# A float32 encoder trunk on one core: gate rows multiplied and split in two lots of four, later pieces of x asked for one block sooner, the residual asked for behind the last key block's weights

## The chip, the core and the metric

The kernel runs on one core of one Trainium2 chip. The metric is the device time of one execution in microseconds (us), less is better. The engines that matter are TensorE (PE; its weight loads are PEld), VectorE (DVE), ScalarE (ACT), GpSimd (POOL) and SyncE (SP), which issues nearly all transfers. [...]

## The reference

Two layers over x (256 tokens, 2048 features, float32). Cut to what matters here:

```python
for l in range(DEPTH):                                   # DEPTH = 2
    h = rms_norm(x, norm1_g[l])
    q, k, v, gu, gv = jnp.split(h @ w_in[l], splits, axis=-1)
    q = apply_rope(rms_norm(q.reshape(B, S, 8, 128), q_norm_g[l]), cos, sin)
    k = apply_rope(rms_norm(k.reshape(B, S, 2, 128), k_norm_g[l]), cos, sin)
    attn = banded_window_attention(q, k, v, sink[l])     # softmax with a sink logit per head
    sgu = chunked_spatial_gating(gelu(gu), gelu(gv), ...)   # gu * (w_s @ layer_norm(gv) + b_s)
    mixed = concatenate([rms_norm(attn, attn_out_g[l]), rms_norm(sgu, sgu_out_g[l])])
    x = x + mixed @ w_o[l]
    x = x + conv_gated_ffn(rms_norm(x, norm2_g[l]), w_up[l], conv_w[l], conv_b[l], w_down[l])
```

## The kernel before, in words

**Products in parts.** Every float32 factor is split in a high part (rounded to fp32r) and a low part (the rest), and a product is three matmuls: high by high, low by high, high by low. Weights come from HBM in blocks of 1 MB (128 x 2048) into four `raw` tiles. ACT copies the high part into `his`, DVE subtracts it and writes the low part into `los` (`lo_part`, L149). For the row products (`rows_by_cols`, L203 for the matmuls by the high part, L208 for those by the low part) a block is split in two halves of 128 x 1024, and `his` and `los` have four such places in a ring: a place is written again when PE has read it. A block covers four key tiles of 128; each takes four L203 and two L208 matmuls of 512 columns.

**Activations.** Left factors are also split, by `split_act`: ACT writes gain times value as the high part (L359), DVE the low part (L360). `first_rows(b)` does so for block b of x in the first layer: x transposed comes in pieces of 256 KB (`in_xT`, L675; the first four smaller, L106).

**The first stage.** In layer 0 the keys and values (`psk`) and the first queries (`psq`) are built side by side over four blocks b of the features (`NB` = 4). Around them stand: a load of the rope tables, of the row `qk` (gains of q and k and the sinks, copied to all partitions, L454) and of the rest of the column parameters, all three issued by ACT and tied by `issue_after` behind the ACT instruction that was the last written there; `rope_tables`, which multiplies those tables out on DVE (L463, L465) and writes `nsink`, the negated sinks (L473); and the residual `xr`, two transfers of 1 MB (L721), whose squares ACT sums for the first norm.

**The gate and the output product.** The mixed rows are multiplied by `w_o` in eight groups: `out_rows(0, c, ra)` for the attention half, c = 0 to 3, then `out_rows(1, c, rs)` for the gating half. Each group takes two blocks of `w_o` and ends in `residual` (L690). `gate(u)`, u = 0 to 3, multiplies two heads of gu by the spatial product (L849) and adds their squares on ACT and DVE (L386, L389, L390). `gained` splits the result into eight left factors for the gating half (L359, L360). `inv_rms_cols` adds up the squares on DVE (L401) and leaves a step that is let in later: two PE transposes of the sums (L407), a reduction on DVE (L409) and a power on POOL; its result is `ra` for the attention rows (sums in `acca`) and `rs` for the gating rows (sums in `accs`).

**What sets the order.** The program is written as Python calls, and a scheduler orders each engine's instructions by priority and by its own estimate of when their inputs are there. `urgent()` raises the priority of what is written under it; `let_in` places deferred steps inside a product. So a moved line changes the order on several engines, and the order is shown below where the prediction rests on it.

Of the kernel before, what the change touches and what calls it, by code (L numbers as in the profile page):

```python
# [53 lines left out]
C_N1, C_AG, C_SG, C_N2, C_CW = 0, 16, 24, 32, 48  # L54
# [6 lines left out]
def encoder(ctx: ExitStack, tc: tile.TileContext, xT, x, w_in, w_gu, w_o, w_up, w_down, wsT, pcol, prow, rope, out):  # L61
# [12 lines left out]
    def sl(shape, dt=F32):  # L74
        return slots.tile(shape, dt, tag="sl", name="sl")
# [13 lines left out]
    def mm():  # L89
        return mmp.tile([P, 2, W], F32, tag="mm", name="mm")  # L90
# [7 lines left out]
    def urgent():  # L98
        return tc.high_priority(offset=AHEAD)
# [8 lines left out]
    with urgent():  # L108
        pc = lay.tile([P, N_COL], F32, tag="pc", name="pc")
# [70 lines left out]
    def latest(engine=mybir.EngineType.PE):  # L180
        return next(i for i in reversed(nc.cur_bb.bb.instructions) if i.engine == engine)
# [14 lines left out]
    def rows_by_cols(ps, acts, src, first, last, raw=None):  # L196

        parts = split_narrow(src, raw)
        for kk in range(KB):
            hi, lo = [p[:, kk % 2 * W : (kk % 2 + 1) * W] for p in parts[kk // 2]]  # L200
            for m in range(2):
                for part in range(2):
                    nc.tensor.matmul(  # L203
                        ps[m], acts[kk][:, part, m * P : (m + 1) * P], hi,
                        start=first and kk == 0 and part == 0, stop=False,
                    )
            for m in range(2):
                nc.tensor.matmul(  # L208
                    ps[m], acts[kk][:, 0, m * P : (m + 1) * P], lo, start=False, stop=last and kk == KB - 1
                )  # L210
            if kk == 1:
                let_in()
# [144 lines left out]
    def split_act(src, g):  # L357
        t = sl([P, 2, SEQ], F32R)
        nc.scalar.activation(t[:, 0, :], src, AF.Copy, scale=g)  # L359
        nc.vector.scalar_tensor_tensor(  # L360
            out=t[:, 1, :], in0=src, scalar=g, in1=t[:, 0, :].bitcast(F32), op0=ALU.mult, op1=ALU.subtract
        )
        return t
# [36 lines left out]
    def inv_rms_cols(acc, n, tag):  # L400
        nc.vector.tensor_tensor(out=acc[:, 0, :], in0=acc[:, 0, :], in1=acc[:, 1, :], op=ALU.add)  # L401
        got = st([P, 2], tag + "r")

        def turned():
            t = tp([P, 2, P])
            for m in range(2):
                nc.tensor.transpose(t[:, m, :], acc[:, 0, m * P : (m + 1) * P], ident)  # L407
            v = st([P, 2], tag + "s")
            nc.vector.tensor_reduce(out=v, in_=t, axis=AX.X, op=ALU.add)  # L409
            inv_rms(v, n, tag, 2, got)  # L410

        waiting.append(turned)
        return got


    def sum_squares(ssq, c, by_vector=False):
        for m in range(2):
            junk = sc([P, W])
            rows = xr[:, m, c * W : (c + 1) * W]
            if by_vector:  # L420
                nc.vector.tensor_tensor_reduce(
                    out=junk, in0=rows, in1=rows, scale=1.0, scalar=0.0,
                    op0=ALU.mult, op1=ALU.add, accum_out=ssq[:, m, c : c + 1],
                )
            else:
                nc.scalar.activation(junk, rows, AF.Square, accum_out=ssq[:, m, c : c + 1])

    def inv_rms_rows(ssq, tag):
        v = st([P, 2], tag + "s")
        nc.vector.tensor_reduce(out=v, in_=ssq, axis=AX.X, op=ALU.add)  # L430
        return inv_rms(v, D, tag, 2)
# [20 lines left out]
    def layer_params_rest(l, pc, eng):  # L452
        qk = lay.tile([P, 264], F32, tag="qk", name="qk")
        eng.dma_start(qk, prow[l : l + 1, 0:264].partition_broadcast(P))  # L454
        eng.dma_start(pc[:, C_CW:], pcol[l, :, C_CW:])
        return qk

    def rope_tables(qk, ropes):
        tabs = []
        for g0 in (R_QG, R_KG):  # L460
            t = sl([P, 2, 2, HD])
            for m in range(2):
                nc.vector.tensor_tensor(out=t[:, 0, m, :], in0=ropes[:, 0, m, :], in1=qk[:, g0 : g0 + HD], op=ALU.mult)  # L463
                for a, b in ((0, 64), (64, 0)):
                    nc.vector.tensor_tensor(  # L465
                        out=t[:, 1, m, a : a + 64],
                        in0=ropes[:, 1, m, a : a + 64],
                        in1=qk[:, g0 + b : g0 + b + 64],
                        op=ALU.mult,
                    )  # L470
            tabs.append(t)
        nsink = lay.tile([P, NQ], F32, tag="nsink", name="nsink")
        nc.vector.tensor_scalar_mul(nsink, qk[:, R_SINK : R_SINK + NQ], -1.0)  # L473
        return tabs, nsink
# [58 lines left out]
    def gained(tiles, g0, pc):  # L533
        return [split_act(t[:, i, :], pc[:, g0 + 2 * j + i : g0 + 2 * j + i + 1]) for j, t in enumerate(tiles) for i in range(2)]
# [90 lines left out]
    qk = None  # L625
# [44 lines left out]
    def first_rows(b):  # L670
        with urgent():
            for j in (2 * b, 2 * b + 1):
                if b:
                    t = sl([P, 2, SEQ])
                    nc.sync.dma_start(t, xT[:, 2 * j : 2 * j + 2, :])  # L675
                else:
                    t = xs[j]
                for i in range(2):
                    c = C_N1 + 2 * j + i
                    hT.append(split_act(t[:, i, :], pc[:, c : c + 1]))  # L680
# [15 lines left out]
    NB = NK // KB  # L696
    for l in range(DEPTH):
        pc, qk = params
        acts = hT

        def in_rows(ps, c, b):
            src = w_in[l, c, :, b * KB * W : (b + 1) * KB * W]
            raw = first_raws.pop(0) if l == 0 and first_raws else None
            rows_by_cols(ps, acts[b * KB : b * KB + KB], src, b == 0, b == NB - 1, raw)


        psk, psq = mm(), mm()
        for b in range(NB):
            if l == 0:
                first_rows(b)  # L710

                with tc.issue_after(latest(mybir.EngineType.Activation)):
                    if b == 1:
                        ropes = const.tile([P, 2, 2, HD], F32, tag="ropes", name="ropes")
                        nc.scalar.dma_start(ropes, rope)
                        qk = layer_params_rest(0, pc, nc.scalar)
            if b == NB - 1:
                if l == 0:
                    with tc.issue_after(latest(mybir.EngineType.SP)), urgent():
                        for m in range(2):  # L720
                            nc.sync.dma_start(xr[:, m, :], x[:, m, :])  # L721
                    for c in range(4):
                        sum_squares(ssq, c)
                tabs, nsink = rope_tables(qk, ropes)
                r1 = inv_rms_rows(ssq, "x")
            in_rows([psk[:, m, :] for m in range(2)], 2, b)
            if l == 0:
                in_rows([psq[:, m, :] for m in range(2)], 0, b)
            elif b == NB - 2:
                in_rows([psq[:, m, :] for m in range(2)], 0, 0)  # L730
# [78 lines left out]
        sg, fs = [], []  # L809
# [37 lines left out]
        def gate(u):  # L847
            with urgent():
                nc.vector.tensor_tensor(out=sg[u], in0=sg[u], in1=fs[u], op=ALU.mult)  # L849
                add_squares(accs, sg[u], u == 0)  # L850
# [16 lines left out]
        gates = []  # L867
# [6 lines left out]
        def out_rows(half, c, r):  # L874
            t = mm()
            ps = [t[:, m, :] for m in range(2)]
            for b in range(2):
                src = w_o[l, c, :, (half * 2 + b) * KB * W : (half * 2 + b + 1) * KB * W]
                rows_by_cols(ps, (atts, gates)[half][b * KB : b * KB + KB], src, b == 0, b == 1)
            residual(ps, c, r)  # L880

        ra = inv_rms_cols(acca, D // 2, "a")
        for c in range(4):
            if c == 1:
                for u in range(4):
                    gate(u)
                with urgent():
                    gates.extend(gained(sg, C_SG, pc))
            if c == 2:
                rs = inv_rms_cols(accs, D // 2, "s")  # L890
            out_rows(0, c, ra)
        for c in range(4):
# [88 lines left out]
        for half, (f0, f1) in enumerate(HALVES):  # L981
# [25 lines left out]
            for group in range(2):  # L1007
# [4 lines left out]
                for n, (cs, ks, sevenfold) in enumerate(blocks):  # L1012
# [26 lines left out]
                    c = cs[0]  # L1039
# [75 lines left out]
```

## Time and profile before

| | |
|---|---|
| median of 3 runs | 1953.72 us (1953.59 to 1954.45) |
| profiled execution: its own time | 1956.62 us |
| profiled execution: its span, first to last instruction | 1953.7 us |
| PE busy | 1946.0 us, 8790 matmuls |
| DVE busy | 1404.9 us (72%) |
| ACT busy | 1340.8 us (69%) |
| HBM read | 378.43 MB, 195 GB/s over the span |

The span is from the first to the last instruction of one execution, and the time of that execution lies 2.9 us above it. In a timeline row stand the start in us, how long it took, the engine, the line, the operation, what is written and read with its shape, how many such instructions were merged, and in brackets how long the engine had been idle and who ended that. A matmul's end is modelled, so matmuls that follow closely overlap in the records: PE counts as busy while its array is merely well fed, and time that PE lost is read from the distance between the starts of its instructions.

### The profile page before, as it was taken

To read this page: it belongs to the slowest core of one execution; us is meant where nothing else is said; L and a number is where in the kernel's file an instruction comes from. 1 tells how busy PE (TensorE), PEld (TensorE's weight loads), DVE (VectorE), ACT (ScalarE), POOL (GpSimd) and SP (SyncE) were. 2 spreads that over 40 slices of the span, in tenths; PEclk is the share of its full clock that TensorE was granted. 3 is DMA by queue.
4 is the path that set the end of the run, shared out by engine and by line. 5 is a ranking of instruction groups with operands and counts; after the bars stand their busy time and mean duration, and the time that the engine had idled before them with its cause. 6 is when DMAs were issued, how large, how long until landed. Compare 5 with 4: busy or idle time off the path is not lost.

```text
span 1953.7 us, 23130 instructions
## 1 busy us (share of the span) xinstructions
PE 1946.0 (100%) x8790; PEld 1614.0 (83%) x8790; DVE 1404.9 (72%) x1732; ACT 1340.8 (69%) x1473; POOL 21.3 (1%) x25
## 2 busy tenths in 40 slices
PE   9999999999999999999999999999999999999999
PEld 7888788888888888888888888888888888888887
DVE  5759775667886666779867796756669856566896
ACT  6776587777755777776776864877776557777753
POOL 0100000000000000000000000000000000000000
PEclk9999999999999999999999999999999999999999
DMA  9764586776556777656767546867775567777563
GB/s 354 219 206 151 178 256 189 220 230 212 185 219 234 205 233 225 216 173 221 236 211 236 158 153 216 235 216 221 221 215 184 221 222 217 215 209 222 173 243 131
DMA packets 191023, 414.03 MB, mean 212 GB/s; under 512 B 139456, under 2 KB 140736, under 8 KB 146112
## 3 DMA queue, kind: packets, MB, share of 16 engines
q1 hardware_dynamic: 190192, 411.83, 66.0%
q8 instruction: 68, 1.11, 0.2%
q10 hardware_dynamic: 720, 0.73, 0.1%
q14 instruction: 43, 0.35, 0.1%
HBM read 378.43 MB, written 2.10 MB: 195 GB/s over the span
## 4 chain that ended last, share of the span: by engine, by line
PE 97%; DVE 1%; ACT 0%; issue 0%; POOL 0%; DVEq 0%
PE mm L221 64%; PE mm L203 12%; PE mm L208 6%; PE mm L336 3%; PE mm L281 2%; PE mm L282 2%; PE mm L287 2%; PE mm L341 2%; PE tp L221 1%; PE tp L287 1%; PE tp L282 1%; PE tp L281 1%; PE tp L379 0%; PE tp L609 0%; PE tp L380 0%; PE tp L381 0%
## 5 line engine op out<-in xcount | busy, mean ns | idle before, releaser
L149 DVE TENSOR_TENSOR los<-raw,his 128x2048 fp32r<-128x2048 f32 (+3 forms) x476 | 867.6, 1833 | 466.3 <-ACT his L175 321.4
L221 PE MATMUL mm<-his,sl 128*128 128x512 f32 x3680 | 872.1, 389 | 0.0
L221 PEld LDWEIGHTS mm<-his,sl 128*128 128x128 f32 x3680 | 690.9, 188 | 143.2
L175 ACT ACTIVATE his<-raw 128x2048 fp32r<-128x2048 f32 (+1 forms) x236 | 446.8, 1895 | 123.0 <-PE mm L221 97.5
L221 PE MATMUL mm<-los,sl 128*128 128x512 f32 x1840 | 454.7, 389 | 0.0
L221 PEld LDWEIGHTS mm<-los,sl 128*128 128x128 f32 x1840 | 345.5, 188 | 71.6
L203 PE MATMUL mm<-his,sl 128*128 128x512 f32 x1152 | 312.2, 392 | 1.4 <-DVE sl L360 1.4
L164 ACT ACTIVATE his<-raw 128x1024 fp32r<-128x1024 f32 (+1 forms) x180 | 186.2, 1039 | 146.7 <-PE mm L203 125.5
L203 PEld LDWEIGHTS mm<-his,sl 128*128 128x128 f32 x1152 | 215.4, 188 | 47.7 <-DVE sl L360 2.9
L506 ACT COPY sl<-sl 128x1024 uint16<-128x1024 uint16 x98 | 132.3, 1350 | 119.0 <-DMA sl<-sl 119.0
L208 PE MATMUL mm<-los,sl 128*128 128x512 f32 x576 | 178.4, 390 | 1.2 <-DVE los L149 1.2
L208 PEld LDWEIGHTS mm<-los,sl 128*128 128x128 f32 x576 | 107.9, 188 | 24.4 <-DVE los L149 2.0
L264 ACT ACTIVATE his<-raw 128x2048 fp32r<-128x2048 f32 x30 | 57.4, 1914 | 63.9 <-DVE raw L263 38.6
L909 ACT ACTIVATE sl<-sl,pc 128x256 f32<-128x256 f32 x176 | 95.2, 589 | 0.9
L930 ACT COPY sl<-sl 128x1024 uint16<-128x1024 uint16 x88 | 92.0, 1046 | 2.7
L910 DVE SCALAR_TENSOR_TENSOR sl<-sl,pc 128x255 f32<-128x255 f32 x176 | 77.1, 477 | 4.5 <-ACT sl L909 4.2
L367 ACT ACTIVATE sl<-sl 128x256 fp32r<-128x256 f32 x88 | 31.9, 409 | 70.4 <-DVE sl L958 70.4
L913 DVE SCALAR_TENSOR_TENSOR sl<-sl,pc 128x255 f32<-128x255 f32 x176 | 77.0, 476 | 0.1
L257 ACT ACTIVATE his<-raw 128x1536 fp32r<-128x1536 f32 x30 | 44.6, 1487 | 28.7 <-PE mm L221 19.1
L928 ACT ACTIVATE sl<-mm,yr 128x512 f32<-128x512 f32 x88 | 59.7, 679 | 4.9 <-PE mm L221 4.9
L336 PE MATMUL mm<-sl,his 128*128 128x512 f32 x256 | 62.1, 392 | 0.0
L281 PE MATMUL mm<-his,sl 128*128 128x512 f32 x154 | 60.1, 390 | 0.0
(148 smaller groups left out, 1306.5 us busy)
## 6 DMA issues: line engine op xcount, KB each, us to landing
raw<-in_w_up SPq DMA_DIRECT2D x176, 1024.0 KB, 5.0
raw<-in_w_down SPq DMA_DIRECT2D x86, 1024.0 KB, 4.6
raw<-in_w_in SPq DMA_DIRECT2D x38, 1024.0 KB, 5.0
raw<-in_w_o SPq DMA_DIRECT2D x32, 1024.0 KB, 4.9
raw<-in_w_gu SPq DMA_DIRECT2D x16, 1024.0 KB, 5.6
sl<-sl SPq DMA_TRANSPOSE x244, 4.4
sl<-in_prow SPq DMA_DIRECT2D x12, 256.0 KB, 7.6
raw<-in_w_in SPq DMA_DIRECT2D x8, 256.0 KB, 5.8
```

The costliest lines, as they stand in the source:

```text
L149: nc.vector.tensor_tensor(out=lo, in0=part, in1=hi.bitcast(F32), op=ALU.subtract)
L164: nc.scalar.activation(hi[:, cs], part, AF.Copy)
L175: nc.scalar.activation(hi[:, :n], raw[:, :n], AF.Copy)
L203: nc.tensor.matmul(ps[m], acts[kk][:, part, m * P : (m + 1) * P], hi, start=first and kk == 0 and part == 0, stop=False,)
L208: nc.tensor.matmul(ps[m], acts[kk][:, 0, m * P : (m + 1) * P], lo, start=False, stop=last and kk == KB - 1)
L221: nc.tensor.matmul(ps[m], acts[kk][:, part % 2, m * P : (m + 1) * P], w, start=first, stop=done and kk == len(acts) - 1 and part == 2,)
L281: nc.tensor.matmul(ps[m], a[0], w[0][:, cs], start=new, stop=False)
L336: nc.tensor.matmul(ps[:, i, :], part_of(0, k, i), x1, start=k == 0, stop=False)
L506: nc.scalar.copy(words, tall.rearrange("p (b a) n -> p b (a n)", b=2))
L909: nc.scalar.activation(t[:, i, :], s[:, i, :], AF.Identity, bias=col(3), scale=col(1))
L910: nc.vector.scalar_tensor_tensor(out=t[:, i, 1:], in0=s[:, i, : SEQ - 1], scalar=col(0), in1=t[:, i, 1:], op0=ALU.mult, op1=ALU.add)
L930: nc.scalar.copy(h, rows.bitcast(U16).rearrange("p (j n b) -> p j b n", j=2, b=2))
```

## The change

Three edits:

- In layer 0 the pieces of x for block b + 1 are asked for and split between the key and the query product of block b. Before, the pieces for block b were asked for ahead of the key product of block b.
- In the last block `rope_tables` is written ahead of the key product, and the load of the residual, its sums of squares and the norm `r1` behind it. Before, all of these stood ahead of it.
- The gate is done in two lots. `gate(0)`, `gate(1)` and their four left factors are written ahead of `out_rows(0, 1, ra)`, `gate(2)`, `gate(3)` and theirs ahead of `out_rows(0, 2, ra)`; `rs` moves from ahead of group c = 2 to ahead of c = 3. Before, all four gates and eight factors stood ahead of c = 1.

```diff
             if l == 0:
-                first_rows(b)
+                if b == 0:
+                    first_rows(0)
 
                 with tc.issue_after(latest(mybir.EngineType.Activation)):
...
+            if b == NB - 1:
+                tabs, nsink = rope_tables(qk, ropes)
+            in_rows([psk[:, m, :] for m in range(2)], 2, b)
             if b == NB - 1:
                 if l == 0:
                     with tc.issue_after(latest(mybir.EngineType.SP)), urgent():
...
-                tabs, nsink = rope_tables(qk, ropes)
                 r1 = inv_rms_rows(ssq, "x")
-            in_rows([psk[:, m, :] for m in range(2)], 2, b)
             if l == 0:
+                if b + 1 < NB:
+                    first_rows(b + 1)
                 in_rows([psq[:, m, :] for m in range(2)], 0, b)
...
-            if c == 1:
-                for u in range(4):
+            if c in (1, 2):
+                us = (2 * c - 2, 2 * c - 1)
+                for u in us:
                     gate(u)
                 with urgent():
-                    gates.extend(gained(sg, C_SG, pc))
-            if c == 2:
+                    for u in us:
+                        gates.extend(gained([sg[u]], C_SG + 2 * u, pc))
+            if c == 3:
                 rs = inv_rms_cols(accs, D // 2, "s")
```

The instructions are the same in kind and count on every engine; their order differs. The changed file is six lines longer, so its line numbers are higher by 4 to 6 behind the edits (L715 becomes L716, L849 becomes L853).

DVE in the first stage of layer 0, before: `raw_231` is the second block of key weights, `raw_261` the second block of query weights, `sl_212` to `sl_223` are pieces of x; the write of `nsink` stands behind both blocks.

```order
L149 TENSOR_TENSOR los_117<-raw_101,his_116 128x512 [waits DMAHW4_49,Activation_49]
L360 SCALAR_TENSOR_TENSOR sl_212<-sl_210,pc_83,sl_212 128x256 [waits DMAHW5_49,Activation_49]
L360 SCALAR_TENSOR_TENSOR sl_215<-sl_210,pc_83,sl_215 128x256 [waits Activation_49]
L149 TENSOR_TENSOR los_117<-raw_231,his_116 128x1024 [waits DMAHW6_49,PE_49,Activation_49]
L149 TENSOR_TENSOR los_117<-raw_231,his_116 128x1024 [waits PE_49,Activation_49]
L360 SCALAR_TENSOR_TENSOR sl_220<-sl_218,pc_83,sl_220 128x256 [waits DMAHW7_49,Activation_49]
L360 SCALAR_TENSOR_TENSOR sl_223<-sl_218,pc_83,sl_223 128x256 [waits Activation_49]
L149 TENSOR_TENSOR los_117<-raw_261,his_116 128x1024 [waits DMAHW0_49,PE_49,Activation_49]
L149 TENSOR_TENSOR los_117<-raw_261,his_116 128x1024 [waits PE_49,Activation_49]
L473 TENSOR_SCALAR nsink_415<-qk_228 128x8 [waits DMAHW3_49]
L149 TENSOR_TENSOR los_117<-raw_307,his_116 128x1024 [waits DMAHW1_49,PE_49,Activation_49]
```

DVE at the same place, now: `raw_277` is the second block of query weights.

```order
L149 TENSOR_TENSOR los_117<-raw_101,his_116 128x512 [waits DMAHW4_49,Activation_49]
L360 SCALAR_TENSOR_TENSOR sl_180<-sl_178,pc_83,sl_180 128x256 [waits DMAHW5_49,Activation_49]
L360 SCALAR_TENSOR_TENSOR sl_183<-sl_178,pc_83,sl_183 128x256 [waits Activation_49]
L473 TENSOR_SCALAR nsink_397<-qk_228 128x8 [waits DMAHW0_49]
L149 TENSOR_TENSOR los_117<-raw_231,his_116 128x1024 [waits DMAHW6_49,PE_49,Activation_49]
L360 SCALAR_TENSOR_TENSOR sl_188<-sl_186,pc_83,sl_188 128x256 [waits DMAHW1_49,Activation_49]
L360 SCALAR_TENSOR_TENSOR sl_191<-sl_186,pc_83,sl_191 128x256 [waits Activation_49]
L149 TENSOR_TENSOR los_117<-raw_231,his_116 128x1024 [waits PE_49,Activation_49]
L149 TENSOR_TENSOR los_117<-raw_277,his_116 128x1024 [waits DMAHW3_49,PE_49,Activation_49]
```

The write of `nsink`, which waits for the transfer of `qk`, has moved up by six rows, ahead of the low part of the second key block.

ACT in the same stage, before: the three parameter loads stand behind the second key block's high parts.

```order
L164 ACTIVATE his_116<-raw_101 128x512 [waits DMAHW4_49]
L359 ACTIVATE sl_212<-sl_210,pc_83 128x256 [waits DMAHW5_49]
L359 ACTIVATE sl_215<-sl_210,pc_83 128x256
L164 ACTIVATE his_116<-raw_231 128x1024 [waits DMAHW6_49,DVE_49,PE_49]
L164 ACTIVATE his_116<-raw_231 128x1024 [waits DVE_49,PE_49]
L359 ACTIVATE sl_220<-sl_218,pc_83 128x256 [waits DMAHW7_49]
L359 ACTIVATE sl_223<-sl_218,pc_83 128x256
L715 DMA ropes_226<-in_rope 128x512
L454 DMA qk_228<-in_prow 128x264
```

ACT at the same place, now.

```order
L164 ACTIVATE his_116<-raw_101 128x512 [waits DMAHW4_49]
L716 DMA ropes_226<-in_rope 128x512
L359 ACTIVATE sl_180<-sl_178,pc_83 128x256 [waits DMAHW5_49]
L359 ACTIVATE sl_183<-sl_178,pc_83 128x256
L454 DMA qk_228<-in_prow 128x264
L455 DMA pc_83<-in_pcol 128x352
L164 ACTIVATE his_116<-raw_231 128x1024 [waits DMAHW6_49,DVE_49,PE_49]
```

The load of `qk` is now issued right behind the first piece of x of the second block, ahead of the second key block's high parts.

DVE in the output product of layer 0, before: `sl_483` is `acca`, whose sum (L401) stands here; the rows behind it are spatial products.

```order
L360 SCALAR_TENSOR_TENSOR sl_1705<-sl_1697,pc_83,sl_1705 128x256 [waits Activation_49]
L836 TENSOR_TENSOR sl_1713<-tp_1708,sl_750 128x2x128 [waits PE_49]
L836 TENSOR_TENSOR sl_1713<-tp_1708,sl_750 128x2x128
L401 TENSOR_TENSOR sl_483<-sl_483 128x256 [waits DVE_49]
L836 TENSOR_TENSOR sl_1746<-tp_1741,sl_750 128x2x128 [waits PE_49]
L836 TENSOR_TENSOR sl_1746<-tp_1741,sl_750 128x2x128
L409 TENSOR_REDUCE as_1752<-tp_1749 128x2 [waits PE_49]
```

DVE there, now: `raw_1903` and `raw_1933` are the blocks of group c = 2, `sl_1575` and `sl_1717` the second lot of gated rows.

```order
L390 TENSOR_TENSOR sl_1162<-sl_1162,sl_1887 128x512 [waits DVE_49]
L360 SCALAR_TENSOR_TENSOR sl_1893<-sl_1575,pc_83,sl_1893 128x256 [waits Activation_49]
L149 TENSOR_TENSOR los_117<-raw_1903,his_116 128x1024 [waits PE_49,Activation_49]
L360 SCALAR_TENSOR_TENSOR sl_1896<-sl_1717,pc_83,sl_1896 128x256 [waits Activation_49]
L360 SCALAR_TENSOR_TENSOR sl_1899<-sl_1717,pc_83,sl_1899 128x256 [waits Activation_49]
L149 TENSOR_TENSOR los_117<-raw_1933,his_116 128x1024 [waits DMAHW4_49,PE_49,Activation_49]
L401 TENSOR_TENSOR sl_483<-sl_483 128x256
L401 TENSOR_TENSOR sl_1162<-sl_1162 128x256 [waits DVE_49]
L409 TENSOR_REDUCE as_1752<-tp_1749 128x2 [waits PE_49]
```

The sum of `acca` has moved down behind both lots of the gate and three of the four low parts of group c = 2.

PE in the same product, now: `mm_1819` is group c = 1, `mm_1902` group c = 2.

```order
L208 MATMUL mm_1819<-los_117,sl_1702 128x512
L203 MATMUL mm_1819<-his_116,sl_1705 128x512 x4
L208 MATMUL mm_1819<-los_117,sl_1705 128x512
L407 MATMUL tp_1749<-ident_118,sl_483 128x128 [waits DVE_49,PE_49]
L407 MATMUL tp_1749<-ident_118,sl_483 128x128
L208 MATMUL mm_1819<-los_117,sl_1705 128x512
L203 MATMUL mm_1902<-his_116,sl_1141 128x512 [waits Activation_49]
```

The transposes of `acca` (L407), which before stood within the last matmuls of group c = 0, now stand at the end of group c = 1.

## The prediction

> **What bounds the kernel now.** I read the page's head and its chain first, then the waits of PE.
>
> ```profile
> span 1953.7 us, 23130 instructions
> PE 1946.0 (100%) x8790; PEld 1614.0 (83%) x8790; DVE 1404.9 (72%) x1732; ACT 1340.8 (69%) x1473; POOL 21.3 (1%) x25
> PE 97%; DVE 1%; ACT 0%; issue 0%; POOL 0%; DVEq 0%
> PE mm L203 <- DVE sl L360: 1.4, 2, 1.2
> PE mm L208 <- DVE los L149: 1.2, 1, 1.2
> ...
> PE tp L609 <- DVE sl L601: 0.4, 1, 0.4
> ```
>
> The chain is PE for 97% of the span. In the list of waits the columns are total us, times, longest: beyond the very start, PE waits twice for more than 1 us. Nothing else can end earlier, so an edit can save only what PE loses now, and costs what PE loses anew. A busy PE is not yet a full one, so I measure it by the distance between starts, for which the chain's longest stretch gives the unit and two windows an occurrence.
>
> ```profile
> 271.83 228.48 PE mm L221 x1008
> 20.00:40.00 20.00, 18.85 (x82) 14.73 (x81) 12.13 (x17) 11.01 (x15) 0.00 (x0) 1.00 0.95 362
> 240.00:260.00 20.00, 20.00 (x90) 16.58 (x89) 14.81 (x22) 15.24 (x16) 0.00 (x0) 1.00 0.62 184
> ```
>
> One matmul of 512 columns costs 228.48 / 1008 = 0.227 us. (The windows' columns are the stretch, its length, busy time and count of PE, PEld, DVE, ACT and POOL, the granted clock, the DMA share and GB/s.) An undisturbed window holds 90 matmuls, the one from 20 to 40 holds 82: 8 x 0.227 = 1.8 us lost there. The timeline shows at what.
>
> ```profile
> 1.05 4.64 PE L117 MATMUL tp<-ones 128*128 128x128 f32 x20 [1.05 <-DVE ones L113]
> 5.34 1.81 PE L203 MATMUL mm<-his,sl 128*128 128x512 f32 x4
> 7.46 1.08 PE L203 MATMUL mm<-his,sl 128*128 128x512 f32 x4
> 9.80 3.24 ACT L164 ACTIVATE his<-raw 128x512 fp32r<-128x512 f32 x5 [0.55 <-DMA raw<-in_w_in]
> 13.44 0.91 ACT L359 ACTIVATE sl<-sl,pc 128x256 fp32r<-128x256 f32 x2 [0.40 <-DMA sl<-in_xT]
> 16.62 0.33 ACTq L715 DMA_DIRECT2D ropes<-in_rope  x1
> 16.98 0.45 ACTq L454 DMA_DIRECT2D qk<-in_prow  x1
> 18.42 0.74 PE L208 MATMUL mm<-los,sl 128*128 128x512 f32 x2
> 28.33 0.17 DVE L473 TENSOR_SCALAR nsink<-qk 128x8 f32<-128x8 f32 x1 [5.70 <-DMA qk<-in_prow]
> 28.44 1.22 DVE L149 TENSOR_TENSOR los<-raw,his 128x1024 fp32r<-128x1024 f32 x1
> 28.57 0.39 PE L203 MATMUL mm<-his,sl 128*128 128x512 f32 x1
> 30.11 0.98 PE L203 MATMUL mm<-his,sl 128*128 128x512 f32 x3 [1.15 <-DVE sl L360]
> ```
>
> DVE stands 5.70 us at the write of `nsink`, until `qk` has landed; everything behind it on DVE stands too, and PE gets its left factor at 30.11, 1.3 us later than the 28.57 + 0.23 at which it was due. The other break is in the gate.
>
> ```profile
> 189.04 1.06 PE L825 MATMUL tp<-sl 128*128 128x128 f32 x8
> 201.84 1.98 PE L203 MATMUL mm<-his,sl 128*128 128x512 f32 x8
> 203.79 3.49 DVE L149 TENSOR_TENSOR los<-raw,his 128x1024 fp32r<-128x1024 f32 x3
> 205.06 0.73 PE L208 MATMUL mm<-los,sl 128*128 128x512 f32 x2 [1.24 <-DVE los L149]
> ```
>
> Eight matmuls from 201.84 on end their turn at 203.65, the next starts at 205.06, when the first low part is there: 1.4 us. So both breaks together hold 1.8 + 1.4 = 3.2 us, which is all that the change can win at these places. That is below 0.2% (3.9 us), about what a measurement of this kernel can tell from no change.
>
> **The first stage: the new place of `nsink`.** `rope_tables` is written sooner, and on DVE the write of `nsink`, with its wait for `qk`, now stands ahead of the low part of the second key block, which PE needs at 18.42 (L208). Behind the waiting write are queued all low parts and left factors; PE's matmuls wait for them, ACT's next high parts for PE. So the question is when `qk` lands. It is issued by ACT, now behind the two L359 that end at 13.44 + 0.91 = 14.35, instead of at 16.98; `ropes` goes ahead of it behind the last small L164, at 9.80 + 3.24 = 13.04. The list of transfers gives size, and us from issue to landing:
>
> ```profile
> q10 hardware_dynamic: 720, 0.73, 0.1%
> ropes<-in_rope ACTq DMA_DIRECT2D x1, 256.0 KB, 7.7
> qk<-in_prow ACTq DMA_DIRECT2D x1, 132.0 KB, 11.3
> pc<-in_pcol ACTq DMA_DIRECT2D x1, 24.0 KB, 2.5
> ```
>
> Three estimates, each an estimate from these rows. If `qk` takes as long as before, it lands at 14.35 + 11.3 = 25.7. If the pair takes as long as before, from the issue of `ropes` at 16.62 to 28.33, it lands at 13.04 + 11.7 = 24.8. If it takes only what `ropes` took, at 14.35 + 7.7 = 22.05. I take their mean, 24.2. From landing to PE: the write to the low part 28.44 - 28.33 = 0.11, the low part 1.22, about 0.06 to PE's start, 1.4 in all. PE goes on at 25.6 instead of 18.42: **+7.2 us**, with ends of 5.0 (22.05) and 8.7 (25.7). The far end is a landing like that of the small `pc`, 14.35 + 2.5 = 16.9, with no wait at all; it is farthest from the row of `qk` itself, and I keep it as a rival. PE has no other work there, since its matmuls are in order and each group needs its low parts. Once the wait is over, the blocks asked for meanwhile have landed, so nothing adds; the old wait at 28.33 is gone, **-1.8 us**.
>
> **The clock behind a long wait.** PE's first four L203 take 1.81 us, the next four 1.08: it starts at a lower rate though the granted clock in the windows is 1.00, and comes to its pace after some 5.7 us from its first matmul at 1.05. Neither break of 1.3 to 1.4 us is followed by slow matmuls; no row shows a break of 7 us. So a break costs between nothing and 5.7 us at half the rate, 2.85 us. A break of 7 us is nearer to a start than to one of 1.4: I take **+2.3 us**. [...]
>
> **The pieces of x and the residual.** The pieces of x go one product sooner past SP's queue, between weight blocks; each is 256 KB against 1 MB, and what they delay by one piece is a block that the wait above makes late to be used: cost nil while that wait stands. The residual's two transfers of 1 MB, asked for behind the key weights, delay query blocks, of which four tiles of 24 matmuls (5.4 us each) are ahead: nil as well. Its squares, seven rows on ACT, stand in a stretch where ACT is busy 11.0 of 20 us. Without that cover each transfer costs at most its 1 MB / 362 GB/s = 2.9 us, once.
>
> **The gate in two lots.** The long row of L360 ahead of the low part at 203.79 is halved, so the old break should go: **-1.4 us**. But the sum of `acca` (L401) now stands on DVE behind both lots and three low parts of group c = 2, and PE's transposes of it (L407) stand at the end of group c = 1, ahead of all of c = 2. DVE's rows in this stretch, by groups (busy, mean ns):
>
> ```profile
> L149 DVE TENSOR_TENSOR los<-raw,his 128x1024 fp32r<-128x1024 f32 x6 | 7.1, 1219 | 0.1
> L360 DVE SCALAR_TENSOR_TENSOR sl<-sl,pc 128x256 fp32r<-128x256 f32 x12 | 5.3, 480 | 0.0
> L390 DVE TENSOR_TENSOR sl<-sl 128x512 f32<-128x512 f32 x5 | 3.4, 686 | 0.0
> L836 DVE TENSOR_TENSOR sl<-tp,sl 128x256 f32<-128x256 f32 x6 | 2.2, 413 | 0.0
> L849 DVE TENSOR_TENSOR sl<-sl 128x512 f32<-128x512 f32 x3 | 2.0, 681 | 0.0
> L815 DVE TENSOR_TENSOR sl<-sl,rb 128x512 f32<-128x512 f32 x1 | 0.7, 683 | 0.0
> L354 DVE TENSOR_TENSOR sl<-mm,sl 128x512 f32<-128x512 f32 x1 | 0.7, 678 | 0.0
> L401 DVE TENSOR_TENSOR sl<-sl 128x256 f32<-128x256 f32 x1 | 0.4, 411 | 0.0
> 188.56 1.06 ACT L164 ACTIVATE his<-raw 128x1024 fp32r<-128x1024 f32 x1 [1.19 <-PE mm L203]
> ```
>
> From the moment at which PE frees the first place of the `los` ring in the first block of c = 1, the new order needs one L164 (1.06) and then on DVE 7 L149 (8.5), 10 L360 (4.8), 4 L390 (2.7), 5 L836 (2.1), 3 L849 (2.0), L354, L815 and L401 (1.8): 23 us with ACT's, or 21.3 if in runs of one kind each is shorter by some 0.06 (three L149 in a run take 3.49, not 3.66). PE meanwhile has 83 matmuls of 0.227 (18.8) and eight small ones like those at 189.04 (about 0.9): 19.7. So L407 waits 1.6 to 3.3 us, and I take **+2.0**, near the shorter end, as runs are common here. With the old break the place gives +0.6, between -1.4 (the sum written sooner than the count says) and +1.9. In layer 1 the sum stands early in both orders, and no wait of this kind was there: nil. In attention, softmax rows change places with split rows of the weights; PE's one listed wait there is 0.4: nil, between -1.0 and +0.5.
>
> **The sum.** +7.2 - 1.8 + 2.3 + 0.6 = +8.3 us on the profiled execution's span of 1953.7, which the execution exceeds by 2.9 outside of its instructions; the median of 1953.72 is 2.9 below that execution, and I add the change to it: **1962.0 us**. The smallest terms together give 5.0 - 1.8 + 0 - 1.4 = +1.8 (1955.5), the largest 8.7 - 1.8 + 2.85 + 1.9 + 0.5 = +12.2 (1965.9).
>
> **The rivals.** *`qk` lands promptly (not slower).* ACT's loads have a queue of their own (q10, 0.73 MB). If it got an equal share, half of 362 GB/s, `ropes` and `qk` (388 KB) would take 2.1 us and the 2.5 of a small load, and land at 13.04 + 4.6 = 17.7; PE would go on at 19.1: +0.7 - 1.8 + 0.6 = -0.5, **1953.2**. [...] Against it speaks the row of `qk`: 388 KB took 11.7 us beside 362 GB/s of weights, 33 GB/s and no half. It decides below a landing at about 22, where the wait is 5.1 or less and the clock holds: +3.9. Chance 0.08. *`qk` lands midway*, at 19.9: a wait of 2.9, too short for the clock: +2.9 - 1.8 + 0.6 = +1.7, **1955.4**, chance 0.08. *The clock holds* through 7 us: 8.3 - 2.3 = +6.0, **1959.7**, chance 0.10; the two short breaks speak for it, the start against it. *Both old breaks go and none comes*, with 1.0 from attention: -1.8 - 1.4 - 1.0 = -4.2, **1949.5**, chance 0.04; this needs a landing before 16.9 and DVE faster than its rows at the gate.
>
> **Numbers.** The forecast has 0.70. Slower by over 0.2% (above 1957.6) are it and the held clock: 0.80; within 0.2% the prompt and the midway landing: 0.16; faster 0.04. The range reaches from 1955, which takes in the midway landing, to 1966, the largest sum.
>
> **What would show it.** In the profile after: DVE L473 waits some 8 to 9 us for `qk` and ends near 24.2; PE L208 waits some 7 us for L149 from 18.4 on; the four L203 behind it take nearer 1.8 than 1.08; L407 waits about 2 us for L401 between 210 and 222; the waits at 28.57 and 203.65 are gone. A `qk` that lands before 20 would make the forecast wrong, a large break in attention or in layer 1 would make it too low.

## The result, and the profile after

The changed kernel takes 1958.36 us (median of 13 runs, 1957.33 to 1960.25) where the kernel before takes 1954.32 (13 runs): +4.0 us, ratio 1.0022 (95% interval 1.0013 to 1.0030). Beside the experiments it was run again: 1958.63 us against 1953.52, +5.1 us, ratio 1.0025 (1.0014 to 1.0036). It is slower, by about half of the 8.3 us forecast; 1958.4 lies inside the range, which was 11 us wide.

The page of the changed kernel, its head and chain, and the list of PE's waits (total us, times, longest):

```profile
span 1956.0 us, 23142 instructions
PE 1946.1 (99%) x8790; PEld 1614.8 (83%) x8790; DVE 1406.1 (72%) x1732; ACT 1343.0 (69%) x1475; POOL 21.3 (1%) x25
PE 98%; DMA 1%; ACT 1%; DVE 0%; issue 0%; SPq 0%; DVEq 0%; ACTq 0%
PE mm L208 <- DVE los L149: 4.1, 1, 4.1
...
PE tp L609 <- DVE sl L601: 0.9, 2, 0.5
```

One wait of 4.1 us stands where there were two of 1.2. The waits at L609 in attention have grown from 0.4 to 0.9 us. PE's busy time is nearly the same as before: it doesn't show the loss. The chain says what the wait hangs on (start, us, what):

```profile
6.80 6.03 DMA sl<-in_xT
12.87 7.96 DMA qk<-in_prow
```

A DMA has come into the chain: a piece of x lands at 12.83, and with it ACT gets to the issue of `qk`, whose landing ends the wait. The timeline of that place:

```profile
12.15 0.35 ACTq L716 DMA_DIRECT2D ropes<-in_rope  x1
...
12.86 0.51 ACT L359 ACTIVATE sl<-sl,pc 128x256 fp32r<-128x256 f32 x1
12.87 0.36 ACTq L454 DMA_DIRECT2D qk<-in_prow  x1
...
17.11 1.07 PE L203 MATMUL mm<-his,sl 128*128 128x512 f32 x4
...
20.85 0.17 DVE L473 TENSOR_SCALAR nsink<-qk 128x8 f32<-128x8 f32 x1 [6.56 <-DMA qk<-in_prow]
20.96 1.22 DVE L149 TENSOR_TENSOR los<-raw,his 128x1024 fp32r<-128x1024 f32 x1
...
22.23 0.91 PE L208 MATMUL mm<-los,sl 128*128 128x512 f32 x2 [4.06 <-DVE los L149]
...
22.94 1.91 PE L203 MATMUL mm<-his,sl 128*128 128x512 f32 x4
24.65 1.05 PE L208 MATMUL mm<-los,sl 128*128 128x512 f32 x2
...
25.50 1.34 PE L203 MATMUL mm<-his,sl 128*128 128x512 f32 x4
...
26.68 0.62 PE L208 MATMUL mm<-los,sl 128*128 128x512 f32 x2
...
27.14 1.07 PE L203 MATMUL mm<-his,sl 128*128 128x512 f32 x4
```

The four matmuls from 17.11 end their turn at 18.02; the next starts at 22.23: 4.2 us lost (the list says 4.1, since it counts from the modelled end of the last matmul). Then come twelve matmuls to 26.68, 4.45 us where 12 x 0.227 = 2.72 are due: 1.7 us more. The row to see is 22.94: four matmuls that took 1.07 before the wait take 1.91 behind it. The window shows it as a granted clock below 1, which none of the windows shown of before has:

```profile
20.00:40.00 20.00, 17.77 (x71) 14.57 (x72) 13.95 (x18) 9.82 (x14) 0.00 (x0) 0.91 1.00 395
```

At the gate the break of 1.4 us is gone, and the transposes of `acca` hardly wait:

```profile
186.81 1.06 ACT L164 ACTIVATE his<-raw 128x1024 fp32r<-128x1024 f32 x1 [4.82 <-PE mm L203]
...
189.78 2.00 PE L829 MATMUL tp<-sl 128*128 128x128 f32 x16
...
206.14 1.23 DVE L149 TENSOR_TENSOR los<-raw,his 128x1024 fp32r<-128x1024 f32 x1 [0.31 <-ACT his L164]
...
207.29 0.75 DVE L401 TENSOR_TENSOR sl<-sl 128x256 f32<-128x256 f32 x2
...
207.52 0.39 PE L208 MATMUL mm<-los,sl 128*128 128x512 f32 x1
...
207.85 0.41 PE L407 MATMUL tp<-ident,sl 128*128 128x128 f32 x2
```

L407 was due at 207.52 + 0.23 = 207.75 and starts at 207.85: 0.1 us. DVE even idles 0.31 us ahead of its last low part.

### The profile page after: what moved, and what is told of

Read it like the earlier page. It is cut to its first block, busy times and chain, and to the rows that moved or that the text cites. A ratio compares the mean times of both kernels' runs of the same rounds, so it can differ in the third digit from the quotient of the medians.

```text
span 1956.0 us, 23142 instructions
## 1 busy us (share of the span) xinstructions
PE 1946.1 (99%) x8790; PEld 1614.8 (83%) x8790; DVE 1406.1 (72%) x1732; ACT 1343.0 (69%) x1475; POOL 21.3 (1%) x25
## 4 chain that ended last, share of the span: by engine, by line
PE 98%; DMA 1%; ACT 1%; DVE 0%; issue 0%; SPq 0%; DVEq 0%; ACTq 0%
PE mm L221 64%; PE mm L203 13%; PE mm L208 6%; PE mm L336 2%; PE mm L281 2%; PE mm L287 2%; PE mm L282 2%; PE mm L341 1%; PE tp L221 1%; PE tp L281 1%; PE tp L282 1%; PE tp L287 1%; DMA sl<-in_xT 1%; PE tp L379 0%; PE tp L609 0%; DMA qk<-in_prow 0%
## 5 line engine op out<-in xcount | busy, mean ns | idle before, releaser
L203 PE MATMUL mm<-his,sl 128*128 128x512 f32 x1152 | 312.4, 392 | 0.3 <-DVE sl L360 0.2
L164 ACT ACTIVATE his<-raw 128x1024 fp32r<-128x1024 f32 (+1 forms) x180 | 186.7, 1039 | 151.9 <-PE mm L203 129.6
L203 PEld LDWEIGHTS mm<-his,sl 128*128 128x128 f32 x1152 | 215.9, 189 | 45.9 <-DVE sl L360 1.0
L208 PE MATMUL mm<-los,sl 128*128 128x512 f32 x576 | 179.0, 391 | 4.1 <-DVE los L149 4.1
L208 PEld LDWEIGHTS mm<-los,sl 128*128 128x128 f32 x576 | 108.3, 188 | 27.1 <-DVE los L149 4.5
```

The costliest lines, as they stand in the source:

```text
L164: nc.scalar.activation(hi[:, cs], part, AF.Copy)
L203: nc.tensor.matmul(ps[m], acts[kk][:, part, m * P : (m + 1) * P], hi, start=first and kk == 0 and part == 0, stop=False,)
L208: nc.tensor.matmul(ps[m], acts[kk][:, 0, m * P : (m + 1) * P], lo, start=False, stop=last and kk == KB - 1)
```

## The experiments

All were timed in five rounds beside the kernel before. Its median was 1953.62 us for the first four, 1953.52 for the second four, 1953.85 for the last four.

**1. The wait taken away.** In the changed kernel, the write of `nsink` goes to an engine with nothing else to do there.

```diff
-        nc.vector.tensor_scalar_mul(nsink, qk[:, R_SINK : R_SINK + NQ], -1.0)
+        nc.gpsimd.tensor_scalar_mul(nsink, qk[:, R_SINK : R_SINK + NQ], -1.0)
```

> The changed kernel with one instruction on another engine: the write of nsink goes from DVE to POOL, which has nothing else to do there; every other instruction keeps its place. Theory (the wait): the loss is DVE's wait for qk, 4.2 us of PE and 1.7 us of slow matmuls behind it; both go, and of the change only what it wins stays: 1.3 us of the old wait at 28.57 and 1.4 us at the gate. 1954.3 - 2.7 = 1951.6 us, ratio 0.9986 (0.998 to 0.9995); PE has no break above 1 us before 60 us. Rival (the transfers): the loss is that pieces of x go past the weight blocks on SP's queue, and qk is only the wait that comes last; then a weight block or a piece of x takes its place, PE still stands 2 to 4 us near 18, and the time stays at 1956 to 1958.4 us, ratio 1.001 to 1.002.

1951.89 us (1951.31 to 1952.12), ratio 0.9991 (0.9982 to 1.0000). In the timeline the transfer lands as late as in the changed kernel, and nobody waits for it but POOL:

```profile
20.76 0.48 POOL L473 TENSOR_SCALAR nsink<-qk 128x8 f32<-128x8 f32 x1 [18.54 <-DMA qk<-in_prow]
```

PE's longest wait past the start is 0.5 us. The whole loss hung on this one instruction of 0.17 us; no weight block and no piece of x took its place, so the rival falls. In the two profiles PE comes to the first transpose of L440, which belongs to the norm of the rows and stands behind the first products, at 80.18 in the changed kernel and at 73.99 here: 6.2 us, of which the rows above give 4.2 of wait and 1.7 of slow matmuls.

**2 and 3. The edits apart.** The third edit alone, the gate in two lots; and the first alone, the pieces of x one product sooner (with rope tables, residual and gate as before).

> The kernel before with the third edit alone: the gate in two lots, rs ahead of group c = 3. Theory after seeing the trace: the break of 1.4 us at 203.65 goes and L407 waits 0.1 us or less: 1954.3 - 1.4 = 1952.9 us, ratio 0.9993 (0.9985 to 0.9998). The prediction's step (L407 waits 2.0 us more than before the edit): +0.6 us, ratio 1.0003. Rival (the other order of attention and gate costs PE more at the transposes L609 than is won): 1954.3 to 1955, ratio 1.000 to 1.0005, with breaks at L609 above 0.5 us each.

> The kernel before with the first edit alone: pieces of x asked for one product sooner; rope tables, residual and gate as before. Theory: the parameter loads are tied to the ACT instruction that was the last written, which this edit moves, and so it alone brings the write of nsink ahead of the second key block's low part: +4.2 - 1.3 + 1.7 = +4.6 us, 1958.9 us, ratio 1.0024 (1.0015 to 1.0032), with the wait of L208 near 18. Rival (it is the second edit, which writes the rope tables ahead of the last key product): the write of nsink keeps its old wait near 28, the time stays within 1 us of the kernel before, ratio 0.9995 to 1.0005.

The gate alone: 1952.07 us (1951.40 to 1953.74), ratio 0.9991 (0.9982 to 1.0000), 1.6 us less, at the edge of what these runs can tell. The first edit alone: 1958.15 us (1956.98 to 1959.35), ratio 1.0025 (1.0015 to 1.0034), 4.5 us more, with the wait of the changed kernel. Two rows of each run, the write of `nsink` in the timeline and PE's longest wait behind its first matmul; of the first edit:

```profile
20.20 0.17 DVE L473 TENSOR_SCALAR nsink<-qk 128x8 f32<-128x8 f32 x1 [6.13 <-DMA qk<-in_prow]
PE mm L208 <- DVE los L149: 3.8, 1, 3.8
```

And of the gate (its 0.5 us are near the start, at 7.4):

```profile
26.36 0.17 DVE L473 TENSOR_SCALAR nsink<-qk 128x8 f32<-128x8 f32 x1 [4.19 <-DMA qk<-in_prow]
PE mm L203 <- ACT his L164: 0.5, 1, 0.5
```

So it is the first edit that moves the parameter loads and with them the write of `nsink`; the rope tables' new place is not needed for it. And in the gate's run the old wait is there, 4.19 us of DVE, but PE loses nothing there: `qk` landed 2 us sooner than in the profiled execution of before.

**4 and 6. PE kept busy in the wait.** Products of the matrix of ones, read by nobody, ahead of the L208 that waits: 12 of them, then 18.

```diff
+            if kk == 0 and fill:
+                with tc.issue_after(latest()), urgent():
+                    idle = tp([P, P])
+                    for _ in range(fill):
+                        nc.tensor.matmul(idle, ones, ones, start=True, stop=True)
             for m in range(2):
                 nc.tensor.matmul(
                     ps[m], acts[kk][:, 0, m * P : (m + 1) * P], lo, start=False, ...
```

> The changed kernel with twelve more products of the 128 x 128 matrix of ones on PE ahead of the L208 that waits for qk (24 small matmuls, an estimate of 2.9 us by the start's 20 in 4.6 us and the transposes' 8 in 1.06 us; their result is read by nobody). PE then idles about 1.3 of the 4.2 us. Theory (the clock falls because PE idles): the matmuls behind the wait keep the distance of 0.227 us, four L203 take 1.08 and not 1.91 us, and 1.7 us are saved: about 1956.7 us, ratio 1.0012. Rival (they are slow for want of data or because DVE's late low parts come one by one): they take 1.9 us as in the changed kernel, and the time stays at 1958.4 us, ratio 1.002.

> The changed kernel with 18 more products of the matrix of ones ahead of the L208 that waits for qk (36 small matmuls; the 24 of the run before took 2.84 us, so 4.3 us). PE then idles at most about 1.4 us, as in the two breaks of the kernel before behind which no matmul was slow. Theory (the clock falls when PE idles for some 2.5 us or more): every run has a mean clock of 1.000, no group of four L203 takes over 1.3 us, and the time is that of the runs with 12 products whose clock held, 1955.0 to 1956.4 us, ratio 1.0007 to 1.0014. Rival (the slow matmuls are not from idling): runs with 0.999 and 0.998 remain, 1958 to 1960.5 us, ratio 1.0025.

With 12: 1958.41 us (1955.04 to 1960.60), ratio 1.0021 (1.0011 to 1.0030), no gain in the median. But its nine runs fall in two groups, by the mean clock that each run lists: four with 1.000 take 1955.0 to 1956.4 us, five with 0.999 take 1958.4 to 1960.6. How long PE waited is on record for the profiled run alone, so part of the distance between the groups may be longer waits. The profiled one is of the second kind:

```profile
18.34 2.84 PE L211 MATMUL tp<-ones 128*128 128x128 f32 x24
22.30 0.17 DVE L478 TENSOR_SCALAR nsink<-qk 128x8 f32<-128x8 f32 x1 [7.74 <-DMA qk<-in_prow]
23.69 0.74 PE L213 MATMUL mm<-los,sl 128*128 128x512 f32 x2 [2.51 <-DVE los L149]
24.27 1.27 PE L203 MATMUL mm<-his,sl 128*128 128x512 f32 x4
...
25.34 1.06 PE L213 MATMUL mm<-los,sl 128*128 128x512 f32 x2
...
26.19 1.91 PE L203 MATMUL mm<-his,sl 128*128 128x512 f32 x4
```

`qk` landed late in it and PE still idled 2.5 us; in this run, with a mean clock of 0.999, 2.5 us were enough. With 18 all eleven runs have a mean clock of 1.000, and no matmul behind the wait is slow:

```profile
18.32 4.18 PE L211 MATMUL tp<-ones 128*128 128x128 f32 x36
22.70 0.73 PE L213 MATMUL mm<-los,sl 128*128 128x512 f32 x2 [0.20 <-DVE los L149]
23.27 1.09 PE L203 MATMUL mm<-his,sl 128*128 128x512 f32 x4
...
24.65 1.07 PE L203 MATMUL mm<-his,sl 128*128 128x512 f32 x4
```

That shows that the slow matmuls came of PE's idling and not of late data: the same low parts come as late as in the changed kernel, the first one written from 21.42 for 20.96. The time is 1957.52 us (1955.30 to 1958.17), ratio 1.0018 (1.0009 to 1.0027), 1.1 below the changed kernel and above the 1955.0 to 1956.4 expected. The extra products also changed the order behind them, and the profile has a wait of its own in the second layer, 1.0 us of PE at L384 for ACT's L378, which the changed kernel has not; that this is all of the 1.1 to 2.5 us above the expectation isn't shown.

**5, 7 and 8. The landing of qk moved.** The changed kernel again; `qk` issued ahead of the rope tables; `qk` issued behind the rest of the column parameters.

```diff
-                        nc.scalar.dma_start(ropes, rope)
-                        qk = layer_params_rest(0, pc, nc.scalar)
+                        qk = lay.tile([P, 264], F32, tag="qk", name="qk")
+                        nc.scalar.dma_start(qk, prow[0:1, 0:264].partition_broadcast(P))
+                        nc.scalar.dma_start(ropes, rope)
+                        nc.scalar.dma_start(pc[:, C_CW:], pcol[0, :, C_CW:])
```

(and in the other the order is `ropes`, `pc`, `qk`.)

> The changed kernel once more, beside the kernels that vary it. Theory (the terms add): gate alone took off 1.5 us and the first edit alone put on 4.5, so 1953.6 - 1.5 + 4.5 = 1956.6 us, ratio 1.0015. Rival (the two edits cost something together, in attention, that neither costs alone): 1957.6 us or more, ratio 1.002, as in its first runs. The mean clock of a run splits them: runs with 0.998 are about 1.7 us longer than runs with 0.999.

> The changed kernel with qk issued ahead of the rope tables on ACT's queue; DVE's order as in the changed kernel, with its wait. Theory (the two loads share what ACT's queue gets, 388 KB in 8.7 us from 12.15 to 20.85, 45 GB/s): qk alone, 132 KB, takes 2.5 + 2.9 = 5.4 us and lands at 17.5, PE waits about 0.9 us (17.5 + 1.4 - 18.0), the clock holds, and the time is that with nsink on POOL plus 0.9: 1952.8 us, ratio 0.9996 (0.999 to 1.0003). Rival (the time of a load there is set by the weights ahead of it and not by the bytes of its queue): qk lands 7 to 8 us after its issue, at 19 to 20, PE waits 2.5 to 3.5 us, the clock falls in some runs, 1955 to 1957 us.

> The changed kernel with qk issued behind the rest of the column parameters, 176 KB more ahead of it; DVE's order as in the changed kernel. Theory (every us by which qk lands later is a us of PE, and the clock is lost once): at 45 GB/s it lands 3.9 us later, near 24.5, PE waits 8 us, and the time is that of the changed kernel plus 3 to 4.5 us: 1960.5 to 1962.5 us, ratio 1.0035 to 1.0045. Rival (by then no weights are on their way, since SP's queue stands behind the same wait, and ACT's loads come fast): it lands about 1 us later, and the time is 1957.5 to 1959 us, ratio 1.002 to 1.0028.

| `qk` | issued | landed | wait of PE | median | ratio |
|---|---|---|---|---|---|
| first | 11.84 | 18.73 | 2.2 | 1955.92 us | 1.0010 (1.0001 to 1.0018) |
| second (the change) | 13.12 | 21.20 | 4.5 | 1958.63 us | 1.0025 (1.0014 to 1.0036) |
| last | 14.03 | 24.72 | 7.3 | 1961.56 us | 1.0042 (1.0028 to 1.0056) |

The rows behind the table's lines in its order, each with the wait of DVE, the wait of PE and what follows:

```profile
11.84 0.35 ACTq L717 DMA_DIRECT2D qk<-in_prow  x1
18.73 0.17 DVE L473 TENSOR_SCALAR nsink<-qk 128x8 f32<-128x8 f32 x1 [4.66 <-DMA qk<-in_prow]
...
20.12 0.73 PE L208 MATMUL mm<-los,sl 128*128 128x512 f32 x2 [2.23 <-DVE los L149]
20.69 1.09 PE L203 MATMUL mm<-his,sl 128*128 128x512 f32 x4
```

```profile
21.20 0.17 DVE L473 TENSOR_SCALAR nsink<-qk 128x8 f32<-128x8 f32 x1 [6.66 <-DMA qk<-in_prow]
...
22.59 1.22 PE L208 MATMUL mm<-los,sl 128*128 128x512 f32 x2 [4.50 <-DVE los L149]
...
28.41 1.07 PE L203 MATMUL mm<-his,sl 128*128 128x512 f32 x4
```

```profile
14.03 0.45 ACTq L719 DMA_DIRECT2D qk<-in_prow  x1
24.72 0.17 DVE L473 TENSOR_SCALAR nsink<-qk 128x8 f32<-128x8 f32 x1 [9.66 <-DMA qk<-in_prow]
...
26.11 1.22 PE L208 MATMUL mm<-los,sl 128*128 128x512 f32 x2 [7.29 <-DVE los L149]
27.13 1.91 PE L203 MATMUL mm<-his,sl 128*128 128x512 f32 x4
```

In these three runs PE waited 0.8 to 0.9 us more for each us by which `qk` landed later: from first to second 2.5 us of landing and 2.3 of wait, from second to last 3.5 us of landing, 2.8 of wait, 2.9 of time, as the last one's theory said. With `qk` first the theory failed (5.4 us to landing, 1952.8 us) and the rival was near: it landed 6.9 us after its issue for 7 to 8, PE waited 2.2 us for 2.5 to 3.5, and the time lies in 1955 to 1957. Its runs fall in two groups again, five with a mean clock of 1.000 (median 1954.22) and six with 0.999 (median 1956.04): 1.8 us apart in one kernel, in which longer waits may have a part. The profiled run, with 2.2 us of wait, is of the first kind: its clock held. In the run of the changed kernel again, three runs with 0.998 take 1959.06 to 1959.93, four with 0.999 take 1957.40 to 1958.63; its median, 1958.63, is 2 us above the 1956.6 expected if the times of the edits added.

**9 to 12. What the rest is worth.** The kernel before with `nsink` on POOL; that with the gate in two lots; the second edit alone; the first experiment again.

> The kernel before with the write of nsink on POOL and nothing else. The prediction's step (the old wait for qk near 28 costs 1.8 us, and its end is a gain): 1953.6 - 1.8 = 1951.8 us, ratio 0.9991. Theory after the run of the gate alone (there the write waited until 26.36 and PE lost 0.1 us, so the 1.3 us at 28.57 was one late execution, 2.9 us above the median): 1953.6 - 0.2 = 1953.4 us, ratio 0.9999 (0.9997 to 1.0001).

> The kernel before with the third edit and nsink on POOL: the changed kernel of the first experiment without its first two edits. Theory (the edits on x and the residual win nothing once nsink waits for nobody, since PE has no break near 20 to 40 in either): within 0.4 us of the changed kernel with nsink on POOL, 1951.9 us, ratio 0.9991. Rival (x asked for sooner wins something at the start): 0.5 us or more above it, 1952.4 us or more.

> The kernel before with the second edit alone: rope tables ahead of the last key product, the residual and its squares behind it. Theory (cost nil, as in the prediction: the write of nsink keeps its place): 1953.6 us, ratio 1.000 (0.9997 to 1.0003). Rival (the residual's 2 MB now go ahead of blocks of weights that come later and make PE wait for one): 1954.5 to 1956.5 us, with a wait of PE for a high or low part between 35 and 60 us.

> The changed kernel with nsink on POOL once more, beside the others: the version that could be kept. Theory: 1951.9 us, ratio 0.9991, mean clock 1.000 in every run. Rival (its first runs were a favourable chip): 1953 us or more.

| kernel | median | ratio |
|---|---|---|
| before, `nsink` on POOL | 1953.80 us | 1.0000 (0.9991 to 1.0009) |
| that and the gate in two lots | 1952.44 us | 0.9992 (0.9983 to 1.0001) |
| the second edit alone | 1951.72 us | 0.9989 (0.9981 to 0.9998) |
| the change, `nsink` on POOL | 1951.80 us | 0.9990 (0.9982 to 0.9999) |

The first line settles the old wait: away with it, and nothing is won. The gate's break stays in that kernel (first fence). In the third both theories fail: the second edit alone is 2.1 us faster. Its write of `nsink` waits 2.90 us on DVE without harm, and the break at the gate is gone although the gate stands in one lot (second fence, DVE there; the third has two rows of the kernel before).

```profile
PE mm L208 <- DVE los L149: 1.3, 1, 1.3
```

```profile
24.45 0.17 DVE L473 TENSOR_SCALAR nsink<-qk 128x8 f32<-128x8 f32 x1 [2.90 <-DMA qk<-in_prow]
...
193.56 2.45 DVE L360 SCALAR_TENSOR_TENSOR sl<-sl,pc 128x256 fp32r<-128x256 f32 x6
...
195.94 3.49 DVE L149 TENSOR_TENSOR los<-raw,his 128x1024 fp32r<-128x1024 f32 x3
...
200.83 0.76 DVE L401 TENSOR_TENSOR sl<-sl 128x256 f32<-128x256 f32 x2
...
204.22 2.73 DVE L690 SCALAR_TENSOR_TENSOR xr<-mm,ar,xr 128x512 f32<-128x512 f32 x4 [0.59 <-POOL ar L396]
```

```profile
193.74 0.41 DVE L401 TENSOR_TENSOR sl<-sl 128x256 f32<-128x256 f32 x1
...
197.50 1.41 DVE L690 SCALAR_TENSOR_TENSOR xr<-mm,ar,xr 128x512 f32<-128x512 f32 x2 [0.59 <-POOL ar L396]
```

The three low parts behind the run of L360 begin at 195.94, where before they began at 203.79. The run of the first edit alone has no break there either. So each of the three edits ends the same 1.4 us, and it can be won only once, which is why the edits' times don't add. The traces show two ways. With the third edit alone the sum of `acca` stays early, and low parts of the weights stand between the two lots of the gate. With the first or the second alone the gate stays in one lot, but the sum of `acca` (L401) and the residual rows that hang on it (L690) stand behind the low parts, where before both stood ahead of them. The late sum, which the prediction booked as a cost, comes with the gain; that it is this row's move which does it wasn't tried. The other 0.7 of the 2.1 us lies ahead of 75 us, where this kernel's profile reaches L440 at 74.29 and that of the first line at 74.97; one profile of each can't tell it from chance. The second line is 0.6 us above the fourth, as its rival said, but the third is as good without pieces of x asked for sooner, so these are not the reason; what it is stays open, and at 0.03% it may be nothing.

## Why the prediction was right, and where its terms were off

The direction, the place and the chain of causes were right: the write of `nsink` stops DVE, the low part comes late, PE stands, and its matmuls are slow for a while behind it. With `qk` last, where it lands at 24.72, near the 24.2 assumed, the kernel takes 8.0 us more than before (1961.56 against 1953.52), for a forecast of 8.3; but it comes to this by other terms, some 7.3 of wait, 1.6 of clock and -1.4 at the gate, so the nearness is in part luck. The change itself took 4.0 to 5.1. Four terms of the sum were mis-sized, and the errors of the last two, +1.8 and -2.0, cancel.

- **The new wait, +7.2: measured 4.2 and 4.7** between starts of matmuls (the second profile's from 17.90 to 22.59). The landing was put at 24.2 and came at 20.85 (21.20 in the second profile). Of the 3.35 us, 1.5 are the issue: I placed it behind the end of two L359 (14.35), but ACT issued it at 12.87, just behind the start of the first of them. The chain shows that it waits for the piece of x, not for ACT's work. The trace of before had it already: there `qk` is written behind two L164 and two L359, and is issued at 16.98, while the second L164 starts at 17.02 and the two L359 at 17.96. The rest is the transfer: 8.0 us where the mean of my three estimates held 9.85. The lower estimate (7.7, that of `ropes`) was the better; the mean leant on two durations of the old place. PE was also due 0.4 us sooner (18.0 for 18.42), which took back a little.
- **The clock, +2.3: measured 1.7 and 2.6** in the two profiles (from 22.59 to 28.41 in the second, 14 matmuls in 5.82 us for 3.18). The prediction let the clock hold for waits of 5.1 us or less, and took 2.9 for too short; both were my estimates, and no run shows them: the clock fell behind 4.1, behind 3.8 in the run of the first edit and behind 2.5 in the profiled run with 12 products, and held behind 2.2 with `qk` first. The half rate of the upper end was my estimate as well; in the first profile four L203 behind the wait take from 22.94 to 24.65, 0.43 us each for 0.227.
- **The old wait, -1.8: nil** (1953.80 without it, 1953.85 with it). This step failed in kind: the 1.3 us break was in the one profiled execution, 2.9 us above the median, in which `qk` landed at 28.33; in the gate's profile it landed at 26.36 and PE lost nothing. I noted that difference, and then still booked the break's end as a gain on the median.
- **The gate, +0.6: measured -1.4** (the break in the profiles; 1.6 in the median of the gate alone). L407 waits 0.1, not 2.0 us. The count of instructions was right, the time was not: from ACT's L164 at 186.8 to the end of the sum near 207.7 DVE needed 20.9 us for the 21.3 taken as its lower bound, and PE had sixteen small matmuls in that stretch and not eight, 0.9 us more of cover.

With the measured terms: 4.2 + 1.7 - 1.4 = 4.5 by the first profile, for +4.0; 4.7 + 2.6 - 1.4 = 5.9 by the second, one of the longer runs, for +5.1. The waits of attention, put at nil, grew by 0.5 us, the upper end given; the first experiment and the second edit alone have them too and are the fastest kernels, so their cost isn't shown.

Of the rivals, prompt service of ACT's own queue fell: 388 KB took from 12.15 to 20.85, 45 GB/s, while all queues together moved 416 GB/s in that stretch. The landing, 20.85, is nearer to the midway rival's 19.9 than to the forecast's 24.2; what sets that rival apart, a clock that holds, did not come. The held clock's time, 1959.7, is the nearest of all to 1958.4, by chance: the clock fell and the wait was shorter.

## What to carry to other kernels

Of a moved load ask who waits for it first, and what stands behind that on its engine: here one write of 8 columns, six rows too early, cost some 6 us (4.2 of wait and 1.7 of slow matmuls), and on POOL it cost nothing (1951.89 us). A break in one profiled execution is worth what it is in the median one: look at where that execution lies among its runs before booking its end as a gain. Where a scheduler orders the work, each edit moves the order everywhere behind it, and several edits may win the same break; run each alone before adding them.

The version to keep is the change with `nsink` on POOL, 1951.80 us, or the second edit alone, 1951.72: 0.1% below the kernel before, with intervals that end just under 1.

## What the runs showed of the hardware

- PE's granted clock fell behind waits (by the lists) of 2.5 us (12 products), 3.8 (the first edit alone), 4.1, 4.5 and 7.3 us (the change, the change again, `qk` last), and held behind 2.2 (`qk` first) and 1.2 us (before), each in one profiled execution, with a mean clock of 0.998 or 0.999 where it fell and 1.000 where it held. By the mean clock that each run lists it fell in 5 of 9 runs with 12 products, in 6 of 11 with `qk` first, and in every run of the kernels with 3.8 us or more. In the profiled ones it cost 1.6 to 2.6 us, by the starts of the matmuls behind the wait against 0.227 us each.
- In the profiled run with 12 products the matmuls became slow after PE had gone back to work, some 4 us after it fell idle: PE idled from 21.2 to 23.7, ran five matmuls at full pace, and was slow from about 25 to 28.
- Transfers of ACT's queue behind each other beside the weights: 132 KB landed 6.9 us after issue (`qk` first, 11.84 to 18.73), 388 KB 8.7 us after the first issue (the change, 12.15 to 20.85), 564 KB 11.9 us (`qk` last, 12.78 to 24.72).
- `qk`, written behind other work on ACT, was issued before that work had run: at 16.98 ahead of rows that start at 17.02 and 17.96 (before), at 12.87 with a row from 12.86 to 13.37 ahead of it (after).
